# One layer of a hybrid diffusion backbone: products with h in scaled float16 pairs, tokens transposed ahead of the conditioning

## Chip, cores and metric

The kernel runs on one core of one Trainium2 chip. The metric is the device time of one execution in microseconds; the time of a kernel is the median of its timed runs. Five engines work side by side and wait for each other by semaphores: TensorE (PE, matrix products; its weight loads are listed apart as PEld), VectorE (DVE), ScalarE (ACT), GpSimd (POOL) and SyncE (SP), which here issues the DMA transfers. Each engine takes its instructions in the order of the program.

## Reference, cut to what matters

One layer for two groups of tokens: 1024 latent tokens (a grid of 16 rows of 64) and 128 context tokens, with 1024 channels.

```python
shift, scale, gate = split(silu(cond) @ w_ada + b_ada, 3)     # cond: c for the latent, c_ctx for the context tokens
h = rmsnorm(x, norm_g) * (1 + scale) + shift
q, k, v, z_a, u_b, z_b, u_c, z_c, g_a, g_b, g_c = split(h @ w_in)   # widths 512 x4, 256 x4, 1024 x3
q = rmsnorm(heads(q), q_g); k = rmsnorm(heads(k), k_g)        # 8 heads of 64
y_a = attend(q, k, v)           # neighbourhood attention and cached context; plain attention for the context tokens
y_b = fourier(u_b, w_fnet)
y_c = pool(u_c, w_pool, pool_scale)
merged = (sigmoid(g_a) * ((silu(z_a) * y_a) @ p_a)
        + sigmoid(g_b) * ((silu(z_b) * y_b) @ p_b)
        + sigmoid(g_c) * ((silu(z_c) * y_c) @ p_c))
return x + gate * (merged @ w_o), k, v
```

Everything is float32, inputs and results.

## The kernel before

Channels or tokens lie on the 128 partitions; the 1152 tokens are 9 tiles of 128 or 3 chunks of 384 (`CH`), and the 1024 channels of h are 8 steps k (`KT`).

**Products in pairs.** A float32 product is made of three products of float32r parts: each operand is split into a rounded part (`hh`, `wh`) and the rest (`hl`, `wl`), and `mm3` (L69 to L71) adds high × high, high × low and low × high in PSUM. `load_unit` (L56) loads a unit of weights (`wr`), casts the high part (L62 on ACT or L64 on DVE) and subtracts for the low part (L65, on DVE or POOL).

**The head.** The conditioning `ada(b)` comes in four blocks b of two k each: its weights `wa` are loaded, split into `wah` (ACT, L273) and `wal` (DVE or POOL in turn, L274), multiplied with both conditioning vectors (L275, L276), the row `ar` is transposed into `pb`, and `ac` gives shift `sh` and scale `gs` of those two k. Each x tile is normed (`xnorm`: squares L238, two steps on POOL, L242). `h_group` transposes x for one k and up to four tiles (L257), ACT applies `gs` and `sh` (L261), DVE splits h into `hh` (L262) and `hl` (L263). `together` interleaves three generators: h of block b, the conditioning of block b + 1 and the products p of block b − 1 for the five first tiles of pair 0. So products start as soon as the first block of h is there.

**Attention.** There are four pairs of heads. A pair's projections p (9 tiles × 8 k × 3 products of 384 columns) give q, k and v of a tile, and `p1_evac` and `p1_norm` take them out of PSUM. Tiles 5 to 7 of pair 0 and tile 8 (`p1_rest`) come after the head. From about 120 us on, items of attention (scores s, exponentials, transposes pt, products po) run with steps of the next pair's projections between them (`fill`); beside the last pair stand products u. `next_weights` (called when 8 steps are left) loads the next unit.

**After the attention** the products z of the branches b and c, pooling and Fourier mixing are made; then the products with p_c and p_b (kept in DRAM), z_a (with `ya`), p_a, and the gates. The gates are 12 units (4 pairs of output tiles × 3 branches) in Winograd's form: seven products of half sizes in place of eight, each 2 × 4 × 3 matmuls of 288 columns (L69 to L71, tile x). h's operands t2, t3 and t4 are made beside p_a (`combos`), the weights' sums s1 to s4 and their parts in `weights_gen`, which runs three operands ahead. Raw weights come from the pool `w2` (`raw_unit`, tag `rw`, 6 buffers of 512 columns), and the raw units of w_o use the same pool. The output projection (`wo`, 432 matmuls of 512 columns) ends the kernel.

Of the kernel before, what the change touches and what calls it, by code (L numbers as in the profile page):

```python
# [31 lines left out]
UOFF = (8, 8 + 1024 + 16)  # L32


@with_exitstack
def mixer_layer(ctx: ExitStack, tc: tile.TileContext, xs, xp, smalls, qgrow, kgrow, bgate, wss, wgate, w1, w3, pw, wo,
# [17 lines left out]
    NB = 9  # L54

    def load_unit(src, n, name, hi_eng=V, lo_eng=V):  # L56
        raw = wp.tile([P, CH], F32, tag="wr", name=f"wr_{name}", bufs=7)
        nc.sync.dma_start(raw[:, :n], src)
        hi = wp.tile([P, CH], F32R, tag="wh", name=f"wh_{name}", bufs=NB)
        lo = wp.tile([P, CH], F32R, tag="wl", name=f"wl_{name}", bufs=NB)  # L60
        if hi_eng is S:
            S.copy(hi[:, :n], raw[:, :n])  # L62
        else:
            hi_eng.tensor_copy(hi[:, :n], raw[:, :n])  # L64
        lo_eng.tensor_tensor(lo[:, :n], raw[:, :n], hi[:, :n].bitcast(F32), op=ALU.subtract)  # L65
        return hi, lo

# [10 lines left out]
    G.memset(ones8, 1.0)  # L78
    mhalf = pers.tile([P, 4], F32, name="mhalf")
    G.memset(mhalf, -0.5)  # L80

    # small vectors, one column each
# [10 lines left out]
    with tc.tile_pool(name="hp", bufs=1, side="right") as hp:  # L93
        hh, hl = [], []
        for i in range(2):
            hh.append(hp.tile([P, 4, NT], F32R, name=f"hh{i}"))
            hl.append(hp.tile([P, 4, NT], F32R, name=f"hl{i}"))
# [4 lines left out]
        late_units = (slice(0, 384), slice(384, 768), slice(768, 1024))  # L102

        def m_units(m, name, **kw):
            return [load_unit(w3[m][:, s_], s_.stop - s_.start, f"{name}_{i}", **kw) for i, s_ in enumerate(late_units)]

        def m_step(pt, wus, c, k):
            a = slice(c * CH, (c + 1) * CH)
            u, j = wus[k // 3], k % 3
            b = slice(j * P, (j + 1) * P)  # L110
            mm3(pt[:, :CH], u[0][:, b], u[1][:, b], hk(hh, k, a), hk(hl, k, a), k == 0, k == KT - 1)
# [5 lines left out]
        with tc.tile_pool(name="qkv", bufs=1) as qkv:  # L117
            p1_state = {}

            def p1_weights(p):  # L120
                return [load_unit(w1[p, k], CH, f"q{p}_{k}", lo_eng=G if k % 2 else V) for k in range(KT)]

            def p1_mm(pt, t, wu, k, first, last):
                a = slice(t * P, (t + 1) * P)
                mm3(pt[:, :CH], hk(hh, k, a), hk(hl, k, a), wu[k][0], wu[k][1], first, last)

            def p1_evac(p, t, pt, vt):
                sq = qkv.tile([P, 256], F32, tag="sq", name=f"sq{p}_{t}", bufs=1)
                S.activation(sq, pt[:, :256], AF.Square, scale=0.125)
# [5 lines left out]
                S.copy(vt["raw"][:, t, :], pt[:, 256:384])  # L135
                V.tensor_reduce(vt["mx"][:, t, :], pt[:, 256:384].rearrange("p (h d) -> p h d", h=2), axis=AX.X, op=ALU.max,
# [6 lines left out]
            def p1_norm(p, t, pt, rs, toks):  # L143
# [10 lines left out]
                # both parts of q, and of k with the first part once more  # L154
# [37 lines left out]
            with tc.tile_pool(name="st", bufs=1) as st:  # L192
# [1187 lines left out]
```

## Time and profile before

| | us |
|---|---|
| timed runs | 997.51, 999.23 (median), 1000.57 |
| span of the profiled execution | 997.4 |
| head, until pair 0's first five tiles leave PSUM | 0 to 83 |
| rest of pair 0, and set-up of the attention | 83 to 120 |
| attention, with projections and u | 120 to about 382 |
| products with p_a | 572 to 622 |
| gates | 622 to 892 |
| output projection | 892 to the end |

The profile's page gives busy times by engine, a coarse course of the span, the chain of waits that ended last, and groups of instructions. A group's row names line, engine, operation and tiles (out<-in), partitions × elements and type, the count, total busy us and mean ns of one, and then the idle time of the engine ahead of it with what ended it. A row of the timeline or of the chain begins with its start and its length in us. Products overlap in PE's pipeline: the duration of one is longer than the step from one to the next, so rates are read from windows and starts. Types are printed as the operand is read: f32 in a product's row also stands for float32r.

### The profile page before, as it was taken

Reading aid. Unit: us, or ns where it says so; the run is one execution under the profiler, and the core shown is the slowest. Engines: PE = TensorE matmul, PEld = TensorE weight load, DVE = VectorE, ACT = ScalarE, POOL = GpSimd, SP = SyncE. Lnnn points to the kernel's source line nnn. Section 1 sums busy time; section 2 is a strip of 40 time slices with the busy share of each in tenths; the row PEclk is TensorE's granted clock in tenths of the full one; section 3 lists DMA queues with packets and bytes.
Section 4 is the critical chain, followed back from the end, with each engine's and each line's share of the span. In section 5 each row is a group of like instructions: output and inputs, shape, how many; then the busy total and the mean of one; then the engine's idle time right before and its main releaser. Section 6 shows DMA issues by size and latency. Waiting matters only on the chain.

```text
span 997.4 us, 17798 instructions
## 1 busy us (share of the span) xinstructions
PE 948.8 (95%) x6532; PEld 870.7 (87%) x6532; DVE 688.4 (69%) x1546; ACT 449.1 (45%) x1003; POOL 202.6 (20%) x308
## 2 busy tenths in 40 slices
PE   3789899999999999989999999999999999999998
PEld 1468788898898999989989999999999999997886
DVE  3897878878878555984634398767677677667422
ACT  5766566767767333353443354333333333333100
POOL 4524545435432120112002200020020010200000
PEclk9899999999999999999999999999999999999999
DMA  8553313302312414122983142535334334349421
GB/s 321 173 165 96 87 36 88 100 26 77 88 42 62 151 52 154 34 78 68 320 292 111 60 137 96 165 100 156 96 94 157 91 114 137 102 130 312 150 95 53
DMA packets 74327, 121.34 MB, mean 122 GB/s; under 512 B 10832, under 2 KB 42492, under 8 KB 74241
## 3 DMA queue, kind: packets, MB, share of 16 engines
q1 hardware_dynamic: 74241, 120.22, 37.8%
q8 instruction: 51, 0.84, 0.4%
q14 instruction: 35, 0.29, 0.1%
HBM read 87.15 MB, written 28.84 MB: 116 GB/s over the span
## 4 chain that ended last, share of the span: by engine, by line
PE 78%; DVE 8%; DMA 4%; POOL 2%; ACT 2%; issue 1%; SPq 0%; ACTq 0%; DVEq 0%; POOLq 0%
PE p L69 4%; PE p L70 4%; PE p L71 3%; PE wo L71 3%; PE wo L70 3%; PE wo L69 3%; PE xc L69 3%; PE xc L70 3%; PE xb L69 3%; PE xa L70 3%; PE xb L70 3%; PE xa L69 3%; PE xa L71 3%; PE xb L71 3%; PE xc L71 3%; PE s L519 3%
## 5 line engine op out<-in xcount | busy, mean ns | idle before, releaser
L69 PE MATMUL p<-wh_q,hh 128*128 128x384 f32 x288 | 110.7, 388 | 0.0
L70 PE MATMUL p<-wl_q,hh 128*128 128x384 f32 x288 | 99.6, 346 | 0.0
L71 PE MATMUL p<-wh_q,hl 128*128 128x384 f32 x288 | 98.1, 342 | 0.0
L69 PEld LDWEIGHTS p<-wh_q,hh 128*128 128x128 f32 x288 | 55.3, 193 | 6.2 <-ACT wh_q L62 0.4
L69 PE MATMUL wo<-woh,mh 128*128 128x512 f32 x144 | 55.8, 391 | 2.1 <-ACT mh L1221 2.1
L70 PEld LDWEIGHTS p<-wl_q,hh 128*128 128x128 f32 x288 | 55.0, 191 | 1.7 <-DVE wl_q L65 0.3
L70 PE MATMUL wo<-wol,mh 128*128 128x512 f32 x144 | 55.5, 390 | 0.0
L71 PE MATMUL wo<-woh,ml 128*128 128x512 f32 x144 | 55.3, 390 | 0.0
L71 PEld LDWEIGHTS p<-wh_q,hl 128*128 128x128 f32 x288 | 54.5, 190 | 0.6
L1160 POOL TENSOR_TENSOR mg<-mg,c11b 128x576 f32<-128x576 f32 x4 | 5.7, 1427 | 237.7 <-DVE c11b L1159 237.7
L523 DVE CUSTOM_DVE_ANT_0 sn<-s,bias 128x512 f32<-128x512 f32 x64 | 43.8, 684 | 13.7 <-PE s L519 12.7
L534 ACT ACTIVATE sn<-sn,mn 128x512 f32<-128x512 f32 x64 | 46.5, 726 | 14.7 <-DVE mn L523 14.2
L547 DVE TENSOR_TENSOR pts<-pt,pts 128x512 f16<-128x512 f32 (+1 forms) x72 | 46.1, 640 | 8.6 <-ACT pts L546 8.3
L1262 DVE TENSOR_TENSOR yo<-wo,gb 128x512 f32<-128x512 f32 x18 | 12.4, 690 | 51.6 <-PE wo L71 51.6
L546 ACT CAST pts<-pt 128x512 f16<-128x512 f32 (+1 forms) x72 | 39.3, 546 | 14.2 <-PE pt L544 10.5
L544 PE MATMUL pt<-ident,sn 128*128 128x128 f32 x256 | 39.6, 274 | 1.2 <-DVE pts L547 1.0
L565 DVE TENSOR_SCALAR yt<-po,ri,un 128x64 f32<-128x64 f32 x72 | 24.4, 339 | 20.2 <-PE po L563 19.4
L134 POOL TENSOR_TENSOR rs<-rs,mhalf 128x4 f32<-128x4 f32 x36 | 37.7, 1048 | 2.9
L69 PE MATMUL u<-hh,wh_u 128*128 128x384 f32 x96 | 35.9, 374 | 0.0
L563 PEld LDWEIGHTS <-pts 128*128 128x128 f16 x792 | 33.0, 98 | 2.9 <-DVE pts L547 0.7
L544 PEld LDWEIGHTS pt<-ident,sn 128*128 128x128 f32 x256 | 30.4, 140 | 4.7 <-DVE pts L547 1.4
L69 PEld LDWEIGHTS wo<-woh,mh 128*128 128x128 f32 x144 | 26.9, 188 | 8.3 <-ACT mh L1221 2.9
(616 smaller groups left out, 3267.6 us busy)
## 6 DMA issues: line engine op xcount, KB each, us to landing
wa<-in_wss_dram SPq DMA_DIRECT2D x16, 512.0 KB
wr_q<-in_w_dram SPq DMA_DIRECT2D x32, 192.0 KB
pp_c<-pec SPq DMA_DIRECT2D x24, 192.0 KB
pp_b<-peb SPq DMA_DIRECT2D x24, 192.0 KB
pp_a<-pea SPq DMA_DIRECT2D x24, 192.0 KB
ppxc<-pp_c SPq DMA_DIRECT2D x16, 288.0 KB
ppxb<-pp_b SPq DMA_DIRECT2D x16, 288.0 KB
ppxa<-pp_a SPq DMA_DIRECT2D x16, 288.0 KB
```

Source lines behind the costliest of these rows:

```text
L69: T.matmul(out, lh, rh, start=first, stop=False)
L70: T.matmul(out, lh, rl, start=False, stop=False)
L71: T.matmul(out, ll, rh, start=False, stop=last)
L134: G.tensor_tensor(rs, rs, mhalf, op=ALU.pow)
L519: T.matmul(pS, c["q"][rb][:, hd, bs], kx[:, hd].rearrange("p (r c) -> p r c", c=64)[:, r0:r0 + 16, KC0[cb]:KC0[cb] + 32], start=(i == 0), ...
L523: V.tensor_tensor_reduce(out=sn, in0=pS, in1=bt.rearrange("p a b -> p (a b)"), op0=ALU.add, op1=ALU.min, scale=1.0, scalar=3e38, accum_out=mn)
L534: S.activation(e[:, :n], it["sn"], AF.Exp, bias=it["mn"], scale=-1.0, accum_out=sm_)
L544: T.transpose(pt[:, j * P:(j + 1) * P], it["e"][:, j * P:(j + 1) * P], ident)
L546: S.copy(pts[:, 0, :n], pt[:, :n])
L547: V.tensor_tensor(pts[:, 1, :n], pt[:, :n], pts[:, 0, :n], op=ALU.subtract)
L563: T.matmul(po[:, :64], it["pts"][:, a, j * P:(j + 1) * P], it["vl"][j][:, c_ * 64:(c_ + 1) * 64], start=(j == 0 and i == 0), stop=(j == nk ...
L565: V.tensor_scalar(yt[:, hd * 64:hd * 64 + 64], po[:, :64], it["ri"], c["un"][:, hd:hd + 1], op0=ALU.mult, op1=ALU.mult)
```

## The change

Operands `hh`, `hl`, the weights of p, u, z and the gates, and t2, t3 and t4 become float16 in place of float32r; `mm3` stays, now on lines L147 to L149. Since float16 has a small range, h is multiplied by one power of two (`shs`) and each unit of weights by another, both worked out on the chip, and the inverse of both is applied where the product leaves PSUM: in `p1_evac`, in `ut`, in silu and in the gates' sigmoid. Products with p_a, p_b and p_c, w_o, the conditioning, Fourier mixing and pooling keep float32r.

A unit's scale is made of sums of squares by partition (ACT, L72, one pass per piece), a product with the 128 × 128 matrix of ones `onesp` in float32 (L83), a sum on DVE (L85), maximum and power −½ on POOL (L86, L87) and a mask that keeps the exponent (`pow2`). There are 28 units: 4 pairs (four pieces of 768 columns), 12 column tiles (u, z) and 12 gate units. `split16` makes the parts: the high part on ACT with the scale (L101), the low part on DVE in one pass (L102), or, for every other piece of a pair, scaled in place on POOL (L97), cast on ACT (L98) and subtracted on POOL (L99). `prep` is a generator, and its steps stand at chosen places ahead of use (`AHEAD`, `m_ahead`, and the steps i of pair 0's rest).

In the head the conditioning runs through all four blocks first; x tiles are normed and transposed into `xT` (L344, L345) between its pieces, in 24 groups. Then `scale_h` works out `shs` from all of `gs` and `sh`, and `make_h(k)` writes `hh` (ACT, L410), h32 (DVE, L411) and `hl` (L413), followed by the products of the five first tiles. x tiles have 5 buffers in place of 9, and h32 uses the same ones.

The gates' raw weights are loaded as 128 × 1024 and two units ahead. `w2` is now closed ahead of the output projection, whose raw weights (`wor`) come from its own pool `fo`.

```diff
-    def load_unit(src, n, name, hi_eng=V, lo_eng=V):
...
+    def squares(pool, raws, name):
+        ss = pool.tile([P, len(raws)], F32, tag="wss", name=f"wss_{name}", bufs=3)
+        for i, r in enumerate(raws):
+            n = r.shape[-1]
+            jk = pool.tile([P, 1024], BF16, tag="wjk", name=f"wjk_{name}{i}", bufs=1)
+            S.activation(jk[:, :n], r, AF.Square, scale=1.0 / 16384, accum_out=ss[:, i:i + 1])
+        return ss
+    def pow2(x):
+        V.tensor_scalar(x.bitcast(I32), x.bitcast(I32), 0x7F800000, None, op0=ALU.bitwise_and)
+    def scale_of(pool, ss, pk, name):
+        n = ss.shape[-1]
+        T.matmul(pk, onesp, ss, start=True, stop=True)
+        sc_ = pool.tile([P, 3], F32, tag="wsc", name=f"wsc_{name}", bufs=4)
+        V.reduce_sum(sc_[:, 2:3], pk, axis=AX.X)
+        G.tensor_scalar(sc_[:, 2:3], sc_[:, 2:3], 1e-36, None, op0=ALU.max)
+        G.tensor_tensor(sc_[:, 0:1], sc_[:, 2:3], mhalf[:, 0:1], op=ALU.pow)
+        pow2(sc_[:, 0:1])
+        return sc_
+    def inverse_of(sc_):
+        V.tensor_tensor(sc_[:, 1:2], sc_[:, 0:1], shs, op=ALU.mult)
+        V.reciprocal(sc_[:, 1:2], sc_[:, 1:2])
+    def split16(hi, lo, raw, sc_, lo_eng=V):
+        if lo_eng is G:
+            G.tensor_scalar(raw, raw, sc_[:, 0:1], None, op0=ALU.mult)
+            S.copy(hi, raw)
+            G.tensor_tensor(lo, raw, hi, op=ALU.subtract)
+            return
+        S.activation(hi, raw, AF.Copy, scale=sc_[:, 0:1])
+        V.scalar_tensor_tensor(lo, raw, sc_[:, 0:1], hi, op0=ALU.mult, op1=ALU.subtract)
+    def prep(pieces, name, lo_engs=(V,)):
...
-            hh.append(hp.tile([P, 4, NT], F32R, name=f"hh{i}"))
-            hl.append(hp.tile([P, 4, NT], F32R, name=f"hl{i}"))
+            hh.append(hp.tile([P, 4, NT], F16, name=f"hh{i}"))
+            hl.append(hp.tile([P, 4, NT], F16, name=f"hl{i}"))
...
-                S.copy(vt["raw"][:, t, :], pt[:, 256:384])
+                S.activation(vt["raw"][:, t, :], pt[:, 256:384], AF.Copy, scale=inv)
...
+                def scale_h():
+                    ab = st.tile([P, 3], F32, name="ab")
+                    V.tensor_reduce(ab[:, 0:1], gs.rearrange("p k c -> p (k c)"), axis=AX.X, op=ALU.max, apply_absolute_value=True)
+                    V.tensor_reduce(ab[:, 1:2], sh.rearrange("p k c -> p (k c)"), axis=AX.X, op=ALU.max, apply_absolute_value=True)
+                    V.scalar_tensor_tensor(ab[:, 2:3], ab[:, 0:1], 32.0, ab[:, 1:2], op0=ALU.mult, op1=ALU.add)
+                    pb = bank("tr", "pbd")
+                    T.transpose(pb[:1, :P], ab[:, 2:3], ident)
+                    m1 = st.tile([1, 1], F32, name="m1h")
+                    V.tensor_reduce(m1, pb[:1, :P], axis=AX.X, op=ALU.max)
...
+                def make_h(k):
+                    h32 = st.tile([P, NT], F32, tag="xt", name=f"h32_{k}", bufs=5)
+                    for a, c in ((slice(0, NS), 1), (slice(NS, NT), 0)):
+                        S.activation(hk(hh, k, a), xT[:, k, a], AF.Identity, bias=sh[:, k, c:c + 1], scale=gs[:, k, c:c + 1])
+                        V.tensor_scalar(h32[:, a], xT[:, k, a], gs[:, k, c:c + 1], sh[:, k, c:c + 1], op0=ALU.mult, op1=ALU.add)
+                    a = slice(0, NT)
+                    V.tensor_tensor(hk(hl, k, a), h32, hk(hh, k, a), op=ALU.subtract)
...
+                wu = run(prep0, 4)
+                scale_h()
...
+                for k in range(KT):
+                    make_h(k)
+                    if k < 6:
                         for t in range(early):
+                            p1_mm(pts[t], t, wu, k, k == 0, False)
...
+                AHEAD = {48: 1, 36: 1, 30: 1, 24: 1, 20: 1, 16: 1, 12: 1, 8: 9}
...
+                if i == 2 and n + 1 < len(units):
+                    gate_scale(n + 1, x[:, 1, QN:QN + 2])
...
+            raw = fo.tile([P, 512], F32, tag="wor", name=f"wor{n}{k}", bufs=6)
+            nc.sync.dma_start(raw, wo[k][:, n * 512:(n + 1) * 512])
```

**The head on PE.** A row names line, operation, tile out<-in, shape, and the engines or DMA queues that it waits for. Before, at the first products of p: `ht` are transposes of x, `p_0_0` is the first tile of pair 0.

```order
L257 MATMUL ht_0_340<-ident,xt_105 128x128
L257 MATMUL ht_0_340<-ident,xt_106 128x128
L69 MATMUL p_0_0_141<-wh_q_0_241,hh_89 128x384 [waits DVE_49,Activation_49]
L69 MATMUL p_0_1_142<-wh_q_0_241,hh_89 128x384
L69 MATMUL p_0_2_143<-wh_q_0_241,hh_89 128x384
L69 MATMUL p_0_3_144<-wh_q_0_241,hh_89 128x384
L257 MATMUL ht_4_313<-ident,xt_108 128x128 [waits DVE_49]
L70 MATMUL p_0_0_141<-wl_q_0_242,hh_89 128x384 [waits DVE_49]
```

Now, at the same place, after the last block of the conditioning (`pa`, `pb`):

```order
L365 MATMUL pa_526<-wah_7_624,sc 4x512
L366 MATMUL pa_526<-wal_7_625,sc 4x512 [waits Pool_49]
L373 MATMUL pb_638<-ident,ar_636 128x4 [waits Activation_49]
L373 MATMUL pb_638<-ident,ar_636 128x4 x3
L394 MATMUL pbd<-ident,ab 1x128 [waits DVE_49,Activation_49]
L401 MATMUL pbs<-m1h,ones_73 128x1 [waits DVE_49]
L147 LDWEIGHTS hh_92 [waits Activation_49]
L147 MATMUL p_0_0_696<-wh_q_650,hh_92 128x384
```

The first product of p has moved from between the first transposes and the second block of the conditioning to behind all of the conditioning and the two products of `scale_h`.

**The gates on PE.** Before, where the third product of a unit of branch c ends and the next begins:

```order
L69 MATMUL xc_8696<-hh_91,wgh_a12c_8628 128x288
L70 MATMUL xc_8696<-hl_92,wgh_a12c_8628 128x288
L71 MATMUL xc_8696<-hh_91,wgl_a12c_8629 128x288
L70 MATMUL xc_8732<-t3l,wgh_s3c_8661 128x288
L71 MATMUL xc_8732<-t3h,wgl_s3c_8662 128x288 [waits DVE_49]
```

Now (a float16 product shows its weight load as a row of its own):

```order
L149 LDWEIGHTS wgl_a12c_8768
L149 MATMUL xc_8839<-hh_94,wgl_a12c_8768 128x288
L83 MATMUL xc_8839<-wss_g_8750,onesp 128x2
L147 LDWEIGHTS wgh_s3c_8804 [waits Activation_49]
L147 MATMUL xc_8883<-t3h,wgh_s3c_8804 128x288
```

The scale product of the next unit stands between two products of this one, in columns of the same PSUM tile that no gate product uses.

**The end on SP.** Before, the queue's rows while the last gate units run (`ppxb` and `ppxa` are products with p, read back; `rw_wo` raw weights of the output projection):

```order
L1008 DMA rw_wo_11691<-in_wo_dram 128x512 [waits DMAHW1_49,DVE_49]
L1153 DMA ppxb_11355<-pp_b 128x576 [waits DMAHW2_49,DVE_49]
L1153 DMA ppxb_11401<-pp_b 128x576 [waits DMAHW3_49,DVE_49]
L1008 DMA rw_wo_11709<-in_wo_dram 128x512 [waits DMAHW4_49,DVE_49]
L1153 DMA ppxb_11441<-pp_b 128x576 [waits DMAHW5_49,DVE_49]
L1008 DMA rw_wo_11721<-in_wo_dram 128x512 [waits DMAHW6_49,DVE_49]
```

Now, after the last `ppxa` (`mr` and `m_d` are the merged tiles, `xr` the residual):

```order
L1373 DMA mr_11955<-m_d 128x576 [waits DMAHW6_49,DVE_49]
L1298 DMA m_d<-mg_11372 128x576 [waits DVE_49]
L1402 DMA xr_0_12019<-in_xs_dram 128x512 [waits Pool_49]
L1352 DMA wor_11921<-in_wo_dram 128x512 [waits DMAHW7_49,PE_49]
L1352 DMA wor_11939<-in_wo_dram 128x512 [waits DMAHW0_49,PE_49]
L1352 DMA wor_11951<-in_wo_dram 128x512 [waits DMAHW1_49]
L1298 DMA m_d<-mg_11412 128x576 [waits DMAHW2_49,DVE_49]
```

The loads of the output projection's weights have moved from among the last gate units to the end of them, and the first two wait for PE.

More of the change, by code (lines that the diff above doesn't have):

```diff
@@ new lines, in split16 @@
+    def split16(hi, lo, raw, sc_, lo_eng=V):
[7 more added lines that the diff above has]
+    def prep(pieces, name, lo_engs=(V,)):
+        unit = {"w": []}
+        raws = []
+        for i, src in enumerate(pieces):
+            n = src.shape[-1]
+            raw = wp.tile([P, WU], F32, tag="wr", name=f"wr_{name}{i}", bufs=8)
+            nc.sync.dma_start(raw[:, :n], src)
+            raws.append(raw[:, :n])
+        yield unit
+        ss = squares(wp, raws, name)
+        yield unit
+        pk = bank("tr", f"pw_{name}")
+        sc_ = unit["sc"] = scale_of(wp, ss, pk[:, :len(raws)], name)
+        unit["inv"] = sc_[:, 1:2]
+        if "ready" in h_scale:
+            inverse_of(sc_)
+        yield unit
+        for i, raw in enumerate(raws):
+            n = raw.shape[-1]
+            hi = wp.tile([P, WU], F16, tag="wh", name=f"wh_{name}{i}", bufs=9)
+            lo = wp.tile([P, WU], F16, tag="wl", name=f"wl_{name}{i}", bufs=9)
+            split16(hi[:, :n], lo[:, :n], raw, sc_, lo_engs[i % len(lo_engs)])
+            unit["w"].append((hi, lo))
+            yield unit
@@ L68, in mm3, with prep_pair, prep_m, run @@
+    def prep_pair(p):
+        return prep([w1[p, i] for i in range(4)], f"q{p}", (V, G))
+    def prep_m(m, name):
+        return prep([w3[m][:, 0:512], w3[m][:, 512:1024]], name)
+    def run(g, n=99):
+        r = None
+        for _ in range(n):
+            x = next(g, None)
+            if x is None:
+                break
+            r = x
+        return r
     def mm3(out, lh, ll, rh, rl, first, last):
@@ L370, in mixer_layer @@
+                p1_norm(0, early - 1, pts[early - 1], rss[early - 1], toks)
                 p1_rest = (wu, vt, toks)
@@ L632, in fill @@
                     for _ in range(n):
[L633 to L634 removed]
+                        if cur["left"] in AHEAD:
+                            ahead(AHEAD[cur["left"]])
                         cur["left"] -= 1
@@ L1128, in all_weights @@
         def all_weights():
-            for u in units:
-                yield from weights_gen(*u)
+            for n in range(len(units)):
+                yield from weights_gen(n)
         wq = all_weights()
@@ L1164, in mixer_layer @@
             for i in range(7):
+                if i == 0 and n + 1 < len(units):
+                    gate_squares(n + 1)
+                if i == 1 and n + 2 < len(units):
+                    gate_load(n + 2)
                 while len(ready) < 3:
```

408 lines of the change are left out of this document (217 added, 191 removed).

## The prediction

> **What bounds the kernel now.** I read the page first (busy shares, clock, chain of waits), then a table of windows by stage, then the timeline where the change acts.
>
> ```profile
> span 997.4 us, 17798 instructions
> PE 948.8 (95%) x6532; PEld 870.7 (87%) x6532; DVE 688.4 (69%) x1546; ACT 449.1 (45%) x1003; POOL 202.6 (20%) x308
> PEclk9899999999999999999999999999999999999999
> PE 78%; DVE 8%; DMA 4%; POOL 2%; ACT 2%; issue 1%; SPq 0%; ACTq 0%; DVEq 0%; POOLq 0%
> ```
>
> PE is busy for 95% of the span at full granted clock, and the chain that ended last lies on PE for 78%. The stages tell where that holds. Columns: stretch, length, busy us (instructions) of PE, PEld, DVE, ACT and POOL, granted clock, DMA share, GB/s.
>
> ```profile
> 12.00:83.00 71.00, 56.22 (x271) 36.17 (x272) 55.04 (x111) 46.19 (x87) 31.30 (x35) 0.93 0.59 207
> 83.00:120.00 37.00, 33.17 (x211) 29.14 (x209) 30.39 (x107) 24.42 (x72) 21.41 (x33) 0.95 0.29 87
> 120.00:420.00 300.00, 294.78 (x2484) 266.06 (x2483) 229.18 (x712) 176.36 (x464) 102.00 (x192) 1.00 0.26 77
> 572.40:621.40 49.00, 49.00 (x284) 49.00 (x283) 45.49 (x113) 26.18 (x62) 1.11 (x1) 1.00 0.34 116
> 700.00:800.00 100.00, 100.00 (x755) 100.00 (x754) 71.72 (x103) 34.39 (x54) 8.12 (x6) 1.00 0.36 109
> 920.00:980.00 60.00, 60.00 (x266) 49.69 (x265) 20.44 (x30) 4.98 (x8) 0.00 (x0) 1.00 0.37 124
> ```
>
> From 120 us on PE has almost no gap. The gates (100 us without one) are bound by nothing but the step from one product to the next. The head, up to 120 us, is shared by all engines.
>
> **Products: float32r against float16.** A full window gives the step as length over count. 384 columns (p_a products): 49.00/284 = 172.5 ns. 288 columns (gates): 100.00/755 = 132.5 ns. 512 columns (output): 60.00/266 = 225.6 ns. From 288 to 512 columns that is 93.1 ns, 0.416 ns a column; what is left over is 12.7 ns a product, whatever its width. What float16 leaves over stands in transposes and products of the attention:
>
> ```profile
> 180.35 0.28 PE L424 MATMUL pk<-id,tok 128*128 128x128 f16 x2
> 180.70 0.54 PEld L424 LDWEIGHTS <-tok 128*128 128x128 f16 x8
> 180.81 0.61 PE L424 MATMUL pk<-id,tok 128*128 128x128 f16 x8
> 181.37 0.43 PE L563 MATMUL po<-vw,pts 128*128 128x64 f16 x9
> 181.63 0.25 PE L563 MATMUL po<-vc,pts 128*128 128x64 f16 x3
> ```
>
> Six steps more take 0.61 − 0.28 = 0.33 us at 128 columns, 55 ns each, and 0.43 − 0.25 = 0.18 us at 64, 30 ns each. At 0.416 ns a column 53.2 and 26.6 ns of that are columns, so 1.8 to 3.4 ns are left over. I take 2.3, a gain of 10.4 ns a product. Beside it stands the weight load:
>
> ```profile
> L563 PEld LDWEIGHTS <-pts 128*128 128x128 f16 x792 | 33.0, 98 | 2.9 <-DVE pts L547 0.7 <-issue 0.5 <-ACT e L534 0.2
> L69 PEld LDWEIGHTS p<-wh_q,hh 128*128 128x128 f32 x288 | 55.3, 193 | 6.2 <-ACT wh_q L62 0.4
> ```
>
> It falls from 193 to 98 ns. In both types it lies beside the product ahead; in the attention, where products are mixed with transposes and waits, the shorter load should free a little more. I take 11.5 ns for the products of 384 columns and 10 for the gates.
>
> The counts: p is 4 pairs × 9 tiles × 8 k × 3 = 864, of which 120 early ones and 96 of pair 0's rest lie ahead of 120 us; u is 288, zc and zb 288, za 288. So 1512 lie behind 120 us. The gates are 12 units × 7 × 2 × 4 × 3 = 2016. Gain: 1512 × 11.5 ns = **17.4 us** and 2016 × 10 ns = **20.2 us**, together 37.6.
>
> **The scales.** Each unit of weights adds a float32 product of `onesp` with the sums of squares. The nearest row is that of `pu`, also float32, a few columns wide, in the stream of p:
>
> ```profile
> 114.90 0.34 PE L69 MATMUL p<-wh_q,hh 128*128 128x384 f32 x1
> 115.17 0.38 PE L457 MATMUL pu<-dg,ones 2*128 2x2 f32 x2
> 115.48 0.45 PE L70 MATMUL p<-wl_q,hh 128*128 128x384 f32 x1
> 115.76 0.34 PE L71 MATMUL p<-wh_q,hl 128*128 128x384 f32 x1
> ```
>
> From the product ahead to the second one behind are 0.86 us, where two steps of 172.5 ns would take 0.35: 0.51 us lost, of which 0.10 is the late second step (0.28 for 0.17). Between float16 weights, which load in half the time, I expect that 0.10 to go: **0.41 us**. Bounds: 0, if it falls into a wait that PE has anyway, and 0.51. Of 28 such products one lies in the head and one in pair 0's rest; 26 × 0.41 = **10.7 us** on PE's path.
>
> The chain behind each (L85, two steps on POOL, `pow2`, inverse) is off PE: weights are prepared a unit ahead, and a gate unit is 168 × 122.5 ns = 20.6 us long. A bank is another matter. The scale product of p, u and z weights writes `tr`, which transposes use too, and it waits for four squares on ACT; all of PE's queue stands behind it. I put **2 us** on such waits over 16 units, between 0 and 0.3 us each, 5 us; the step ahead of each is a whole piece of the schedule.
>
> What loads ACT and DVE: in the gates, squares (2 × 1.24 us a unit by the row of `xsq` below), hi parts with a scale on ACT, and lo parts as scalar_tensor_tensor:
>
> ```profile
> L469 DVE SCALAR_TENSOR_TENSOR v<-vraw,sc,v 128x576 f16<-128x576 f32 x8 | 6.2, 816 | 1.1 <-ACT v L468 0.8
> L134 POOL TENSOR_TENSOR rs<-rs,mhalf 128x4 f32<-128x4 f32 x36 | 37.7, 1048 | 2.9
> ```
>
> 512 of 576 columns: 725 ns against some 680 now, and five small steps a unit; DVE goes from 72% to about 80% of a gate stage that is 8% shorter. PE stays the bound, so this costs nothing. Without that cover it is the fourth rival.
>
> **The head.** The first evacuation of pair 0 stands at 83.0 us:
>
> ```profile
> L129 ACT ACTIVATE sq<-p x36: 362/383/404, 83.0 to 305.1; 128x256 f32<-128x256 f32 x36
> L273 ACT CAST wah<-wa 128x512 fp32r<-128x512 f32 x32 | 18.8, 616 | 12.3 <-DMA wa<-in_wss_dram 6.2 <-DVE wal L274 3.1 <-PE pa L275 2.8
> L238 ACT ACTIVATE xsq<-xt 128x1024 f32<-128x1024 f32 x9 | 9.5, 1055 | 0.2
> L238 ACT ACTIVATION_READ_ACCUMULATOR xsq<-xt 128x1 f32 x9 | 1.7, 188 | 0.0
> L546 ACT CAST pts<-pt 128x512 f16<-128x512 f32 (+1 forms) x72 | 39.3, 546 | 14.2 <-PE pt L544 10.5
> L261 ACT ACTIVATE h<-ht,sh,gs 128x512 f32<-128x512 f32 (+1 forms) x24 | 15.8, 670 | 14.1 <-PE ht L257 6.4 <-DVE hl L263 6.1 <-DVE gs L293 1.5
> L263 DVE TENSOR_TENSOR hl<-h,hh 128x512 fp32r<-128x512 f32 x16 | 14.1, 889 | 0.3
> L242 DVE TENSOR_SCALAR xt<-xt,xrs 128x1024 f32<-128x1024 f32 x9 | 6.8, 754 | 7.3 <-POOL xrs L241 6.5 <-DMA wa<-in_wss_dram 0.8
> ```
>
> Now no product of p can start until all four blocks of the conditioning are through, since one scale of h needs every shift and scale. ACT's row up to the last copy of the conditioning: 16 `wah` × 0.616 = 9.9; 9 norms × 1.24 = 11.2; 24 copies of `xT`, 16 × 0.55 and 8 short ones at about 0.3, 11.2; five squares of 768 columns at about 1.0 and four hi parts at about 0.85 (by width from `xsq`), 8.4; eight small copies, 3. That is 43.7 us from 8 us on. Waits come on top: `wah` alone waited 12.3 us now, 6.2 of it for its transfer. With 10 to 13 us of waits the last block is ready at 62 to 65 us. Then the scale of h, some ten dependent steps on DVE, two on PE, 4 to 5 us, so h starts at 66 to 70. Behind it eight steps of k. PE needs 15 products × 162 ns = 2.4 us for each. DVE needs two passes over 1152 columns: 0.85 us by `xt` (754 ns for 1024), and a subtraction of 1.6 (`v`, 816 for 576) to 2.0 us (`hl`, 889 for 512). With 2.5 us a step, 20 us, the first evacuation comes at 86 to 90 us, some 5 later than now.
>
> Pair 0's rest gives that back. There DVE's weight work stands on the chain of waits:
>
> ```profile
> 104.25 0.47 DVE wl_q L65
> 104.72 0.60 DVE wh_q L64 x3
> 105.45 0.54 DVE wl_q L65
> 105.99 1.36 DVE wh_q L64 x2
> 107.35 1.26 DVE wl_q L65
> ```
>
> These 4.2 us leave DVE's row there: hi parts move to ACT, half the lo parts to POOL. With 96 products × 10.4 ns = 1 us, and ACT taking part of it as a new wait, I expect 4 us back. The net of the head is **+1**, from −5 to +10 (the ends: h at 62, with the waits that ACT has now hidden, and at 75, if the five x loads that now wait for transposes to free a buffer, and POOL's way of splitting pair 0's weights, get in ACT's way).
>
> **Two joints.** From the p_a products to the gates PE waited little; the first gate weights now stand behind the last copies of `pea` on ACT and behind two differences on DVE: +0.7 us (0 to 3). At the end:
>
> ```profile
> 891.52 0.29 PE L71 MATMUL xa<-hh,wgl_s4a 128*128 128x288 f32 x1
> 892.52 0.73 PE L69 MATMUL wo<-woh,mh 128*128 128x512 f32 x2 [0.71 <-ACT mh L1221]
> 167.65 2.09 DMA wr_q<-in_w_dram
> ```
>
> The gap is now 1.0 us. The raw units of w_o were loaded beside the gates, from a pool that lived on; now they come from the pool of the last stage, whose space is that of the operands of the gates. The load waits for PE's last products, SP's queue stands behind it, and PE waits for a transfer (2.1 us) and a cast (0.62) in place of 0.71: **+2 us** (0 to 5).
>
> **Sum.** 997.4 − 37.6 + 10.7 + 2 + 1 + 0.7 + 2 = 976.2 us of span. The timed runs stood at 997.51 to 1000.57 with a median of 999.23, 1.8 above the span: **978 us**.
>
> **Rivals.** (1) *Float16 leaves as much over as float32r*, because a weight load does not vanish behind so short a product. Then 997.4 + 10.7 + 4.7 + 1.8 = 1014.6 us, slower. It decides from a gain under (10.7 + 4.7)/3528 = 4.4 ns a product. For it: no row shows a float16 product of 384 or 288 columns with a new weight each. Against it: the eight transposes above each load a new weight and step at 55 ns, so a load of 98 ns does overlap. Chance 0.06. The Trainium skill, "TensorE: Matmul & The Clock Gate", "Back-to-back issue gap", speaks for this rival: in streams of load and product it has 81 ns a product at 128 columns where a lone one takes 56, 25 ns for the load. By that rule a product of 288 columns would take about 147 ns, an estimate, and the change would lose; the 55 ns of the eight transposes here contradict it.
>
> (2) *Scales hidden, head shorter.* Scale products at 0.2 us (half the gap is shared) give 5.5 back, the waits for the bank 2, and the head at −5 another 6: 978 − 13.5 = 964.5 us. For it: DVE and ACT in the attention are at 76% and 59% and lose weight casts. Chance 0.2.
>
> (3) *The head becomes one long wait.* h starts at 75, no product covers it: the head costs 10, 978 + 9 = 987 us. For it: ACT's row has 44 us of work where its share is 65% now, and every step crosses PE, ACT, DVE and POOL. Chance 0.16.
>
> (4) *DVE or ACT holds PE in gates or attention*, and half of the gates' gain goes: 978 + 10 = 988 us. For it: 80% of DVE is an average with waits in it. Chance 0.1.
>
> **How the numbers follow.** The forecast itself, 971 to 984, has 0.48; rival 1 has 0.06, 2 0.2, 3 and 4 0.26. The range 959 to 993 takes in cases 2, 3 and 4 and the bounds of the scales (0 to 0.51) and joints; about 0.2 lies outside: rival 1, and sums of two cases. A measurement can tell 0.3%, 3 us, from no change. Slower than 1002 is rival 1, 0.05; within 3 us, a mild form of it or 3 and 4 with the joints, 0.04; faster 0.91.
>
> **What would show it.** Windows over whole gate units: a step near 122.5 ns, against 132.5 if rival 1 holds; p_a products unchanged at 172.5. Around `xc<-wss_g` about 0.4 us between gate products. The first `sq<-p` at 86 to 90 us, and the first scores near 120; rival 3 has the first at 95 or later. Idle PE in the attention behind `pw` tiles over 0.3 us, or in the gates behind `wgl`, would be term four or rival 4. A gap of 3 us ahead of the first `wo` is the last term. A step that falls by less than 4 ns makes the whole wrong.

## The result, and the profile after

The changed kernel takes 1044.99 us (median of four runs, 1044.53 to 1046.75) against 998.86 us: a ratio of 1.046, 95% interval 1.044 to 1.0476. It is slower by 46 us, and the forecast was 978. The page of the profiled execution, whose span is 1043.2 us:

```profile
span 1043.2 us, 17932 instructions
PE 927.9 (89%) x6591; PEld 687.4 (66%) x6591; DVE 687.6 (66%) x1600; ACT 532.6 (51%) x1147; POOL 255.0 (24%) x381
PEclk9859999899999999989799998999999999999999
PE 61%; DVE 12%; POOL 7%; DMA 4%; ACT 3%; issue 2%; SPq 0%; DVEq 0%; ACTq 0%; POOLq 0%
```

PE has less work than before (927.9 us for 948.8) and is busy for 89% of the span in place of 95%. POOL has risen from 2% to 7% of the chain of waits, DVE from 8% to 12%. So products became shorter and waits appeared. The windows of the stages (length; busy us of PE, PEld, DVE, ACT, POOL; granted clock; DMA share; GB/s):

```profile
0.00:78.00 78.00, 41.89 (x161) 19.47 (x161) 41.92 (x99) 45.87 (x94) 42.20 (x51) 0.77 0.64 234
96.40:139.00 42.60, 32.84 (x218) 19.18 (x216) 24.77 (x95) 29.96 (x78) 25.52 (x34) 0.92 0.25 80
139.00:417.00 278.00, 249.37 (x2254) 169.32 (x2253) 186.43 (x641) 187.08 (x487) 113.75 (x208) 0.98 0.24 63
700.00:800.00 100.00, 100.00 (x823) 80.12 (x821) 81.93 (x130) 51.10 (x78) 16.74 (x18) 1.00 0.39 122
```

In the attention PE is now idle for 28.6 of 278 us; before, 5.2 of the 262 us from 120 to 382. In the gates it has no gap, and 813 gate products (823 records, ten of which belong to scale products) fit in 100 us where 755 did. By the starts of the first and the last product of each stage (us, of the two profiled executions):

| stretch | before | after | change |
|---|---|---|---|
| start to the first evacuation of pair 0 | 83.0 | 96.4 | +13.4 |
| from there to the first scores | 36.5 | 43.4 | +6.9 |
| attention, first to last scores | 262.0 | 277.1 | +15.1 |
| on to the end of Fourier mixing | 82.1 | 86.7 | +4.6 |
| gap ahead of the products with p_c (`ppc`) | −1.1 | 11.5 | +12.6 |
| these products and the gate row, up to `za` | 57.6 | 58.5 | +0.9 |
| `za` | 51.7 | 47.8 | −3.9 |
| gap ahead of `ppa` | 0.2 | 6.6 | +6.4 |
| `ppa`, up to the first gate product | 49.9 | 54.1 | +4.2 |
| gates | 269.6 | 248.9 | −20.6 |
| gap ahead of the first output product | 1.0 | 7.2 | +6.2 |
| output projection | 100.0 | 100.0 | 0 |

The sum is 45.8, as much as lies between the spans. The row of the attention is read from the first and the last scores, before and after:

```profile
L519 PE MATMUL s<-ka,q x64: 376/389/391, 119.5 to 381.5; 128*128 128x512 f16 x64
L632 PE MATMUL s<-ka,q x64: 379/379/380, 139.7 to 416.8; 128*128 128x512 f16 x64
```

Where PE waits for no chain of small steps (gates, `za`) the change brings what was forecast; every other stretch but the output projection loses.

**The products.** The timeline of PE in the gates, with the scale product of the next unit:

```profile
712.02 0.29 PE L148 MATMUL xb<-hl,wgh_a12b 128*128 128x288 f16 x1
712.14 0.29 PE L149 MATMUL xb<-hh,wgl_a12b 128*128 128x288 f16 x1
712.26 0.28 PE L83 MATMUL xb<-wss_g,onesp 128*128 128x2 f32 x2
712.40 0.28 PE L147 MATMUL xb<-t3h,wgh_s3b 128*128 128x288 f16 x1
712.53 0.28 PE L148 MATMUL xb<-t3l,wgh_s3b 128*128 128x288 f16 x1
```

Steps are 0.12 us, and the scale product takes 0.14 us of PE (712.26 to 712.40).

**The head.** The timeline of POOL:

```profile
58.85 0.90 POOL L87 TENSOR_TENSOR wsc_q<-wsc_q,mhalf 128x1 f32<-128x1 f32 x1
59.72 1.27 POOL L364 TENSOR_TENSOR wal<-wa,wah 128x512 fp32r<-128x512 f32 x1
60.97 4.52 POOL L97 TENSOR_SCALAR wr_q<-wr_q,wsc_q 128x768 f32<-128x768 f32 x2
65.46 1.65 POOL L364 TENSOR_TENSOR wal<-wa,wah 128x512 fp32r<-128x512 f32 x1
67.07 2.36 POOL L99 TENSOR_TENSOR wl_q<-wr_q,wh_q 128x768 f16<-128x768 f32 x1
69.39 1.26 POOL L364 TENSOR_TENSOR wal<-wa,wah 128x512 fp32r<-128x512 f32 x1
```

POOL has no gap from 58.85 to 72.25 us. The last two `wal` of the conditioning stand behind pieces of pair 0's weights, 2.26 us for a scaling and 2.36 for a subtraction, and the conditioning's last product waits for the last of them (70.7 us). The first product of p comes at 78.0.

**The attention.** The chain of waits at one of PE's two stalls of over 5 us (start, length, what), and ACT's row there:

```profile
174.38 1.60 POOL wl_q L99
175.99 0.03 issue
176.01 6.11 DMA wr_m<-in_w_dram
182.12 0.02 issue
182.14 0.68 ACT wjk_m L72 x2
182.82 0.14 issue
182.96 0.72 ACT wjk_m L72 x2
183.67 0.19 ACT tok L250
```
```profile
182.14 0.63 ACT L72 ACTIVATE wjk_m<-wr_m 128x512 bf16<-128x512 f32 x1 [6.80 <-DMA wr_m<-in_w_dram]
```

POOL's subtraction frees a raw buffer, the load of the next unit starts only then, and ACT stands for 6.8 us at a square of that unit. Behind the square stand the casts of `tok` and `pts`, behind these DVE and PE.

**The gap ahead of `ppc`**, in the chain of waits:

```profile
500.61 4.82 POOL tl L829 x4
505.43 0.20 POOL wsc_m L86
505.63 0.07 issue
505.70 0.58 POOL wsc_m L87
506.28 0.02 issue
506.30 0.15 DVE wsc_m L77
...
509.83 2.72 DVE wl_m L102 x3
512.56 0.08 DVE wsc_m L77
...
514.08 0.74 DVE wl_m L102
514.82 0.21 DVE oh_pc L62
515.04 0.04 issue
515.08 0.69 PE ppc L147
```

Three scales of `za` units stand there one behind the other. POOL's steps wait for `tl`, DVE's masks wait for POOL, and the cast of `oh_pc`, for which PE waits, is the last in DVE's row.

### The profile page after: what moved, and what is told of

Its sections match the earlier page's. It is cut to its first block, busy times and chain, and to the rows that moved or that the text cites. A ratio compares the mean times of both kernels' runs of the same rounds, so it can differ in the third digit from the quotient of the medians.

```text
span 1043.2 us, 17932 instructions
## 1 busy us (share of the span) xinstructions
PE 927.9 (89%) x6591; PEld 687.4 (66%) x6591; DVE 687.6 (66%) x1600; ACT 532.6 (51%) x1147; POOL 255.0 (24%) x381
## 4 chain that ended last, share of the span: by engine, by line
PE 61%; DVE 12%; POOL 7%; DMA 4%; ACT 3%; issue 2%; SPq 0%; DVEq 0%; ACTq 0%; POOLq 0%
PE wo L147 3%; PE wo L148 3%; PE wo L149 3%; PE xc L149 3%; PE xb L147 3%; PE xb L149 3%; PE xb L148 3%; PE xc L147 3%; PE xc L148 3%; PE xa L147 2%; PE xa L149 2%; PE xa L148 2%; POOL rs L225 2%; DVE sn L636 2%; DVE pts L660 2%
## 5 line engine op out<-in xcount | busy, mean ns | idle before, releaser
L147 PE MATMUL p<-wh_q,hh 128*128 128x384 f16 x288 | 96.7, 336 | 3.5 <-ACT hh L410 1.9
L148 PE MATMUL p<-wl_q,hh 128*128 128x384 f16 x288 | 96.5, 335 | 0.0
L149 PE MATMUL p<-wh_q,hl 128*128 128x384 f16 x288 | 94.7, 332 | 0.0
L147 PE MATMUL wo<-woh,mh 128*128 128x512 f32 x144 | 56.9, 395 | 7.0 <-ACT woh L1353 7.0
L149 PE MATMUL wo<-woh,ml 128*128 128x512 f32 x144 | 56.4, 394 | 0.0
L238 DVE SCALAR_TENSOR_TENSOR tk<-p,rs,grow 128x64 f32<-128x64 f32 x144 | 31.8, 275 | 37.2 <-POOL rs L225 37.2
L86 POOL TENSOR_SCALAR wsc_g<-wsc_g 128x1 f32<-128x1 f32 x12 | 2.6, 216 | 218.5 <-DVE wsc_g L85 218.5
L636 DVE CUSTOM_DVE_ANT_0 sn<-s,bias 128x512 f32<-128x512 f32 x64 | 43.7, 683 | 11.4 <-PE s L632 11.2
L1407 DVE TENSOR_TENSOR yo<-wo,gb 128x512 f32<-128x512 f32 x18 | 12.4, 691 | 55.7 <-PE wo L149 55.7
L147 PEld LDWEIGHTS <-wh_m 128*128 128x128 f16 x288 | 28.7, 100 | 24.3 <-ACT wh_m L101 5.9
L147 PEld LDWEIGHTS <-hh 128*128 128x128 f16 x288 | 29.2, 101 | 22.4 <-DVE tk L238 3.0
L676 PEld LDWEIGHTS <-pts 128*128 128x128 f16 x792 | 35.1, 99 | 13.4 <-DVE pts L660 7.5
L149 PEld LDWEIGHTS <-wl_m 128*128 128x128 f16 x288 | 28.3, 99 | 20.4 <-DVE wl_m L102 1.5
L676 PE MATMUL po<-vw,pts 128*128 128x64 f16 x576 | 34.1, 195 | 8.4 <-DVE pts L660 5.3
L149 PEld LDWEIGHTS <-hl 128*128 128x128 f16 x288 | 28.8, 100 | 19.0 <-issue 1.8
L148 PEld LDWEIGHTS <-wh_m 128*128 128x128 f16 x288 | 28.5, 99 | 19.0 <-issue 2.4
L148 PEld LDWEIGHTS <-hh 128*128 128x128 f16 x288 | 28.9, 100 | 17.3 <-issue 1.9
```

The source lines that it names most:

```text
L147: T.matmul(out, lh, rh, start=first, stop=False)
L148: T.matmul(out, lh, rl, start=False, stop=False)
L149: T.matmul(out, ll, rh, start=False, stop=last)
L238: ins = V.scalar_tensor_tensor(tkv[:, g], pt[:, g * 64:g * 64 + 64], rs[:, g:g + 1], toks["g"][:, g], op0=ALU.mult, op1=ALU.mult)
L636: V.tensor_tensor_reduce(out=sn, in0=pS, in1=bt.rearrange("p a b -> p (a b)"), op0=ALU.add, op1=ALU.min, scale=1.0, scalar=3e38, accum_out=mn)
L676: T.matmul(po[:, :64], it["pts"][:, a, j * P:(j + 1) * P], it["vl"][j][:, c_ * 64:(c_ + 1) * 64], start=(j == 0 and i == 0), stop=(j == nk ...
```

## Experiments

All times are medians of timed runs with the kernel before beside them (999 to 1001 us); ratios are to it, with their 95% interval. "Attention" is the time from the first to the last `s<-ka`.

**1. No split on POOL.**

```diff
-        return prep([w1[p, i] for i in range(4)], f"q{p}", (V, G))
+        return prep([w1[p, i] for i in range(4)], f"q{p}", (V,))
```

> The changed kernel, but all four pieces of a pair's weights are split on ACT and DVE (lo_engs of prep_pair is (V,)), none on POOL. Theory P (the split on POOL, 2.2 us for the scaling and 1.6 to 2.4 us for the subtraction of a piece, holds up what waits for POOL: wal in the head, rs in every tile's evacuation, free raw buffers): the first product of p moves from 78 us to about 70, the first scores s<-ka from 139.7 to 118 to 122, the two idle stretches of 5 us ahead of py in the attention go, and the time falls from 1045 to 1015 to 1022 us. Theory C (the chains of scales, squares on ACT and small steps, hold up the engines): the first scores stay within 3 us of 139.7 and the time within 5 us of 1045, or above it, since DVE takes eight passes of about 1 us more.

1034.46 us, ratio 1.034 (1.0312 to 1.0366): 10.5 us less, between the two theories. The first scores came at 131.0 us (139.7), the first product of p at 74.9 (78.0), but the attention stayed at 274.3. POOL's pieces cost some 9 us up to the first scores; to take them out does not by itself clear the stalls of the attention (5 comes back to this).

**2. Constant weight scales.**

```diff
-        ss = squares(wp, raws, name)
         yield unit
-        pk = bank("tr", f"pw_{name}")
-        sc_ = unit["sc"] = scale_of(wp, ss, pk[:, :len(raws)], name)
+        sc_ = unit["sc"] = wp.tile([P, 3], F32, tag="wsc", name=f"wsc_{name}", bufs=4)
+        G.memset(sc_, 1024.0)
```

and the same in the gates.

> The changed kernel with a constant in place of each weight scale: the squares, the 28 scale products and the steps on DVE and POOL behind them are left out; the split on POOL stays. Theory P: the pieces on POOL still stand ahead of wal and rs, so the first scores come at 130 to 138 us and the attention stays above 270 us; the gap ahead of ppc shrinks from 8.3 to about 3 us and that ahead of ppa from 6.4 to about 4.5; with 26 scale products at 0.14 us the time is 1022 to 1034 us. Theory C: most of the 46 us goes, 1005 us or less.

1017.28 us, ratio 1.018 (1.0159 to 1.0204): 27.7 us less, more than theory P allowed and less than C. The attention fell to 259.0, the gap ahead of `ppc` from 11.5 to 7.1 (counted from the last product of Fourier mixing; the 8.3 of the expectation counts from the last scale product). The first scores did not move (140.0), although the first evacuation came 5.4 us later (101.8). So, each taken alone, the computed scales cost in the attention and behind it, POOL's split ahead of it.

**3. Both together.**

> No split on POOL and constant weight scales together (squares, scale products and the steps behind them are left out). If the two costs are separate, 1045 - 10.6 - 27.7 = 1007 us, between 1003 and 1010; the first scores come at 129 to 132 us and the attention takes 255 to 259 us. If POOL's pieces hurt only by standing among the steps of the scales, 1013 us or more.

1007.01 us, ratio 1.0066 (1.0043 to 1.009): the two costs add up to within 0.3 us, well inside the spread of its runs (1002.59 to 1012.33). First scores 132.3, attention 258.3.

**4. What in the scales costs.** Three runs. First, raw buffers of their own for u and z, so that their loads do not wait for the pairs:

```diff
-            raw = wp.tile([P, WU], F32, tag="wr", name=f"wr_{name}{i}", bufs=8)
+            raw = (late["wpm"] if name[0] == "m" else wp).tile([P, 512 if name[0] == "m" else WU], F32, tag="wr", name=f"wr_{name}{i}", bufs=6 if name[0] == "m" else 8)
```

> The changed kernel, but the raw weights of u and z have six buffers of their own (a pool opened behind the head) in place of sharing eight with the pairs. Theory Q (in the attention ACT stands at a square whose raw weights have not come, because their load waits until the split of a pair frees a buffer: 6.8 us at 175 to 182 us and as much at 252, and PE's clock halves behind the stall): the squares find their data, both stalls go, the attention from first to last s<-ka falls from 277 to 262 to 266 us, and the time to 1029 to 1034 us. Rival (the chain of a scale itself, its product, POOL's steps and the mask on DVE, costs the 18 us that the constant saved there): the attention stays above 273 us and the time at 1040 us or more.

1048.99 us, ratio 1.0484 (1.0463 to 1.0505): theory Q fell. The attention took 275.3 us. The wait moved: ACT still stood 9.4 us at squares whose load had not landed (seven times, up to 4.5 us), since the scheduler had put each square right behind its load again.

Second, the squares where the program has them:

```diff
-            S.activation(jk[:, :n], r, AF.Square, scale=1.0 / 16384, accum_out=ss[:, i:i + 1])
+            tc.keep_in_program_order(S.activation(jk[:, :n], r, AF.Square, scale=1.0 / 16384, accum_out=ss[:, i:i + 1]))
```

> The changed kernel, with every square of the weights kept at its written place in ACT's order (before, the scheduler had moved it up, right behind the issue of its load). Theory R (ACT stands at a square until its load has landed, 4 to 7 us each time, whichever buffer it waits for; tok, pts and with them PE wait behind it): the two stalls ahead of py go, the attention from first to last s<-ka falls from 277 to 262 to 266 us and the time to 1028 to 1034 us. Rival (the chain of the scale costs, not the squares' place): above 273 and 1040 us.

1034.84 us, ratio 1.0332 (1.0317 to 1.0347), 10.2 us less. ACT no longer waited at a square and the stalls ahead of `py` were gone. But the attention only came to 270.3, with 12.4 us of PE waiting for `pts`; the gap ahead of `ppc` gave another 6.7 us (4.8 in place of 11.5), as the three scales of `za` no longer stood together there, while the stretch from the attention to the end of Fourier mixing took 2.9 us more.

Third, the squares left in, the rest constant:

> The changed kernel with constant weight scales again, but with the squares left in, where the scheduler puts them; scale products and the steps behind them are left out. Theory R: the squares alone keep most of the loss, so the attention stays above 270 us (259 with neither) and the time at 1030 us or more. Rival (products, POOL's steps and the mask cost): 262 us or less, and 1017 to 1023 us.

1021.83 us, ratio 1.021 (1.0184 to 1.0236), attention 259.0: as without squares. A square by itself costs nothing there. With no chain behind it the split comes sooner, the raw buffer is free sooner, and the load has landed when ACT gets to the square (6.4 us of waits in place of 13.2, the longest 1.6). So the long waits at a square take both, an early square and a late buffer. The run is 4.5 us slower than 2 all the same: its first scores came 3.6 us later (143.6).

**5. All of it with computed scales.** No split on POOL, the squares in place, the raw weights of w_o in a pool open beside the gates and p_a's cast on ACT:

> Computed scales, no split on POOL, squares at their written place, raw weights of w_o in a pool open beside the gates and p_a's cast on ACT. If theories P and R hold and add up: 1034.5 for no split on POOL, 13 us less for the squares, 4 for w_o, 3 for p_a: 1014 us, between 1010 and 1019; attention 258 to 263 us. If the chain of scales still costs, 1022 us or more.

1011.68 us, ratio 1.0102 (1.0087 to 1.0117). The row of the scores:

```profile
L635 PE MATMUL s<-ka,q x64: 376/379/380, 130.4 to 390.0; 128*128 128x512 f16 x64
```

390.0 − 130.4 = 259.6 us: without POOL's pieces and with the squares in place, computed scales cost the attention no more than constant ones (258.3). Each of the two alone had given 2.8 and 6.8 us; together they gave 17.5. With the squares in place, POOL's pieces thus still cost the attention 10.7 us (270.3 for 259.6). The traces of these two runs show the way: without the pieces DVE's waits for the steps `rs` on POOL fell from 29.1 to 19.6 us, ACT's waits for DVE ahead of `tok` from 31.7 to 24.1, and PE's waits for `pts` from 12.4 to 6.7.

**6. The joints.** The raw weights of w_o early:

```diff
+        wrp = ctx.enter_context(tc.tile_pool(name="wrp", bufs=1, **TW))
...
-            raw = fo.tile([P, 512], F32, tag="wor", name=f"wor{n}{k}", bufs=6)
+            raw = wrp.tile([P, 512], F32, tag="wor", name=f"wor{n}{k}", bufs=6)
```

> The changed kernel with the raw units of w_o in a pool of their own that is open beside the gates, so that their loads need not wait for the space of the gates' operands. If the gap of 6.9 us between the last gate product and the first output product is that load (4.9 us) and what queues behind it, the gap falls to about 1 us and the time to 1038 to 1040 us. Rival: the gap is the merging of the last tiles on DVE and ACT, and the time stays at 1043 to 1046 us.

1041.2 us, ratio 1.0413 (1.0398 to 1.0429), 3.8 less; the gap ahead of `wo` fell from 7.2 to 3.3 us, not to 1. With constant scales and no split on POOL, the same, raw weights of p_a, p_b and p_c in a pool that opens behind the head, and p_a's cast on ACT:

> As the run without POOL's split and with constant scales, and three more: raw weights of w_o in a pool open beside the gates, raw weights of p_a, p_b, p_c in a pool opened behind the head, and the cast of p_a's high part on ACT as before the change. If the gaps at the three joints come from loads that wait for space and from the cast behind DVE's queue: the gap ahead of ppc falls from 7 to 1 us, that ahead of ppa from 6 to 3, that ahead of wo to 3, and the time to 992 to 997 us. If the tails of the stages ahead (tl on POOL, the differences d on DVE) set them, 1000 us or more. What is left against the 959 us of float16 in the old order is then the head and what DVE and ACT do in the attention.

1007.39 us, ratio 1.0067 (1.0047 to 1.0087): no gain over 1007.01. The gaps did shrink (`ppc` 7.1 to 4.4, `ppa` 6.1 to 1.6, `wo` 8.0 to 3.3), but 9.5 us came back between the first `ppc` and the first `za`, where PE now waited for the copies `peb` on ACT (9.1 us). ACT's row shows them behind the stores of the copies before (`pp_c`), for which it waited 22.9 us there and 14.3 in 3; why the stores held it longer was not tried. The same, but with computed scales, the squares where the scheduler wants them, and four raw buffers of their own for u and z:

> All scales computed as in the changed kernel, with no split on POOL, four buffers of their own for the raw weights of u and z, early raw weights of w_o, p_a, p_b and p_c, and p_a's cast on ACT. Theories P, Q and the joints together: 1045 - 10.6 - 13 - 3.8 - 3 = 1014 us, between 1009 and 1018; the gap ahead of ppc stays at 6 to 8 us, since three chains of scales still stand ahead of the cast on DVE there. If the chains cost by themselves, 1022 us or more.

1025.2 us, ratio 1.0262 (1.0232 to 1.0292), attention 264.6: in the attention the squares' place is worth 5 us more than the buffers. Of the 13.5 us that this run takes longer than 5, 9.3 lie between the first `ppc` and the first `za`, as in the run before. In 5, with p_a's cast on ACT but its load where the change has it, the gap ahead of `ppa` was 6.0; here, with the load early, 1.6. So the load's place decides that gap, not the engine of the cast.

**7. The head.** h takes the constant scale 1, so that it and its products go between the pieces of the last block (scales constant, no split on POOL; `scale_h` is left out, and the transposes and the preparation of pair 0's weights come earlier):

```diff
-                scale_h()
...
+                    if i == 12:
+                        pts = [bank(ebank[t], f"p1_0_{t}") for t in range(early)]
+                    for k in {12: (0,), 13: (1, 2), 14: (3,), 15: (4, 5)}.get(i, ()):
+                        make_h(k)
+                        for t in range(early):
+                            p1_mm(pts[t], t, wu, k, k == 0, False)
```

> No split on POOL and constant weight scales (1007 us), and a head in which h has the constant scale 1, so that h of the first six k and their products are written between the pieces of the conditioning's last block instead of behind it. Theory H (one scale of h for all four blocks puts 24 to 29 us of products behind the end of the conditioning, where there were 14 before): the first evacuation comes at 83 to 87 us in place of 95.5, the first scores at 120 to 125, and the time falls to 995 to 999 us. Rival (ACT and DVE are full there, so the conditioning ends later by as much): the first evacuation above 92 and the time above 1003 us.

996.57 us, ratio 0.9962 (0.9945 to 0.9978): 10.4 us less than run 3, and a little faster than before the change. The first evacuation came at 89.7 us (95.7), the first scores at 123.8 (132.3). The conditioning ended later (77.3 for 66.3 us), but only 12.4 us lay between its last product and the first evacuation in place of 29.4. Theory H held for the sum; the first evacuation was later than it said. What the order gives and what it gives to leave out `scale_h` are not told apart.

**8. The type alone.** The kernel before with float16 for h, the weights that meet h, and t2 to t4, with no scales, in its own order of work:

```diff
-            hh.append(hp.tile([P, 4, NT], F32R, name=f"hh{i}"))
-            hl.append(hp.tile([P, 4, NT], F32R, name=f"hl{i}"))
+            hh.append(hp.tile([P, 4, NT], F16, name=f"hh{i}"))
+            hl.append(hp.tile([P, 4, NT], F16, name=f"hl{i}"))
```

and so for `wh`, `wl`, `wgh`, `wgl` (p_a, p_b and p_c stay float32r) and `tw`.

> The kernel before with float16 in place of float32r for h, the weights that meet h and t2 to t4, with no scales at all and its own order of work (range is left unguarded: small low parts lose bits). This is the type alone. If the step of a product (162.3 and 122.2 ns as in the changed kernel) carries over: 3528 products behind the head at 10.3 ns, 36 us, so 960 to 965 us. Rival: DVE, whose work stays, becomes the bound in the attention or the gates, 975 us or more.

959.37 us, ratio 0.9595 (0.958 to 0.961): the fastest of all, 40 us below before and 86 below the change. Its window over the attention and one in the gates:

```profile
117.50:365.50 248.00, 242.38 (x2228) 166.35 (x2226) 201.01 (x668) 162.05 (x436) 97.48 (x188) 0.99 0.27 78
650.00:750.00 100.00, 100.00 (x819) 79.88 (x817) 79.56 (x116) 36.62 (x58) 7.32 (x5) 1.00 0.43 134
```

The attention takes 248.1 us (262.0 before), the gates 248.8. It leaves float16's range unguarded, so it prices the type and cannot stand in for the change.

## Why the prediction was wrong

**The product term was right.** 10.4 ns a product was read from rows of 64 and 128 columns (the sum took 11.5 and 10); the steps after are 162.3 and 122.2 ns, 10.2 and 10.3 less. The gates gained 20.6 us, and run 8 shows 40 us for all of it, where the term said 37.6 without a head. Rival 1 was rightly set low. The Trainium skill, "TensorE: Matmul & The Clock Gate", "Back-to-back issue gap", gives a stream of load and product about 81 ns a product at 128 columns, but also about 131 ns at 512. Rival 1 carried the 25 ns of the first figure over to 288 columns and left out the second, so its 147 ns are not that section's rule. By the section's formula for a lone product, 288 columns take 122.5 ns, an estimate. The 122.2 ns of the stream here agree with that formula; the 131 ns at 512 columns were not seen, as two `s` products of 512 float16 columns start 216 ns apart.

**The scale product was priced too high.** 0.14 us was measured and 0.41 taken: 26 of them would be 3.6 us, not 10.7. The row of `pu` from which I took the price stood in a stream of float32r. This error made the forecast too slow, so all the others weigh more.

**The step that failed is the cover of the scales.** The text said "The chain behind each (L85, two steps on POOL, `pow2`, inverse) is off PE: weights are prepared a unit ahead", and put 2 us on waits; with the products the sum had 12.7 us for the scales. Shares of busy time stood for the cover (DVE 76%, ACT 59%). But an engine takes its row in order, so a step that waits holds all that is behind it, whatever its share, as ACT's square did for 6.8 us. Constant scales gave 27.7 us back (run 2). In the two profiled executions, 31 us apart, 18 of that lie in the attention, 7 from there to the end of Fourier mixing, and 4 ahead of `ppc`, where DVE stood at masks. The waits at squares are not all of the 18: without them the attention still took 270.3 us, and only without POOL's pieces as well did it come to 259.6. I had named the square in front of `tr` and PE, not the casts behind it on ACT. Nor had I read from the order of the changed kernel that squares stand right behind their loads.

**POOL's split was a bound of a range and not a term.** It stood among the ends of the head ("POOL's way of splitting pair 0's weights get in ACT's way"). Run 1 shows about 9 us up to the first scores and 10.5 in all, and not through ACT: `wal` and the steps `rs` are POOL's own, in one row behind 2.2 us a scaling and 1.6 to 2.4 us a subtraction. "[H]alf the lo parts to POOL" was counted as relief for DVE, and the 4 us that pair 0's rest was to give back became 6.9 us lost.

**The head.** 86 to 90 us for the first evacuation was 96.4, and 92.9 without POOL's split. The rest goes with the order, conditioning first and products behind it, and with `scale_h`: run 7 put the products between the pieces of the last block, left `scale_h` out, and gained 10.4 us. Its mechanism was in the text and its price too small: +1 stood in the sum for +20.2 up to the first scores.

**The joints.** The gap ahead of `wo` was forecast with its mechanism (the load behind PE's last products) at +2 and is +6.2: the load took 4.9 us, where I took 2.1 from a load of another size in another stage, and the run with these weights loaded early (6) gave 3.8 back. The gaps ahead of `ppc` and `ppa`, together +19 us, were not in the sum at all: I had looked at the joint from p_a to the gates (+0.7 forecast, 1.4 found), not at the stages ahead of it that load through `load_unit`'s new pools.

**Rivals and range.** Rival 3 (head) and rival 4 (DVE or ACT holds PE) both came true, rival 4 in the attention and not in the gates that it was priced by; the head cost 20.2 us up to the first scores and the attention 15.1, for their 10 each. They were priced one at a time; "sums of two cases" were left outside the range, although the chains above show one cause, waits in rows that are in order, in both.

What stays open: run 7 has neither computed scales nor POOL's split, and its profiled execution is still 41 us behind that of the type alone. The three gaps ahead of `ppc`, `ppa` and `wo` hold 20.6 of that (7.2, 6.1 and 7.6 us; in run 8 each is 0.1 or less), the attention 11.4 (259.5 for 248.1), the stretch up to the first scores 6.3. In run 7's attention PE waits for `pts` and for transposes behind it; which of ACT's new passes delays them was not tried. Of the gap of 7 us ahead of `ppc` that is left with constant scales, the trace of run 3 shows the last wait: DVE's cast of `oh_pc` stands 2.4 us until its load `or_pc` has landed.

## What to carry to other kernels

Price a change of type and the machinery around it apart, and run the type alone first: here it gives 4%, and the machinery takes it back twice over. A small step that waits costs what stands behind it in its engine's row, so read the row, not the share of busy time; work that is placed as soon as its load is issued makes the engine wait for the load. And work moved to an engine with time to spare is dear if short steps that others wait for go through the same row.

## What was not expected of the hardware

- POOL's scaling of 128 × 768 float32 in place (one input) took 2.2 to 2.3 us in eight cases, longer than its subtraction of two inputs of that size into float16 (1.64 us in the middle of eight, 2.36 at most).
- A stall costs PE more than its length: behind the stall of 5.5 us in the attention and the gap of 6.6 us ahead of `ppa` the granted clock (third number from the end) was 0.50 for some 4 us:

```profile
184.50:188.00 3.50, 3.44 (x23) 2.54 (x24) 2.23 (x8) 3.50 (x13) 2.32 (x6) 0.50 0.00 0
628.00:632.00 4.00, 4.00 (x13) 3.92 (x14) 4.00 (x11) 0.86 (x2) 0.00 (x0) 0.50 0.18 66
632.00:640.00 8.00, 8.00 (x47) 8.00 (x46) 7.71 (x20) 3.55 (x8) 0.00 (x0) 1.00 0.52 178
```

The first `ppa` products ran at half the step rate. The chain there, where 0.17 us was usual before:

```profile
627.99 0.66 PE ppa L147
628.65 0.32 PE ppa L148
628.97 0.32 PE ppa L147
629.29 0.32 PE ppa L149
```

`ppa` takes 52.6 us in place of 49.8 with the same products. In the attention PE is busy for 248.5 us, and in run 5, with the same products, for 243.4, at a granted clock of 0.98 and 1.00: some 5 of the 17.5 us between them are slower products and not idle time. The mean granted clock of the execution is 0.952 against 0.990.
- A square on ACT with its scale as an operand of one value per partition (`inv`) took 474 ns for 128 × 256, and 383 ns with a constant:

```profile
L220 ACT ACTIVATE sq<-p,inv x36: 453/474/504, 96.4 to 344.7; 128x256 f32<-128x256 f32 x36
```
